# Three modulation pieces as row sums, whole-row ring places, a later overflow branch and a new order of the first latents

## The chip, the core and the metric

The program runs on one core of one Trainium2 chip. The metric is the device time of one execution in microseconds, the median of several runs; less is better. TensorE (PE), VectorE (DVE), ScalarE (ACT), GpSimd (POOL) and SyncE (SP, which only issues DMAs here) run their own instruction queues and meet at semaphores.

## What is computed

Two blocks, on 256 latent tokens and 256 context tokens of width 1024, all in fp32. The first has two layers; each takes a modulation vector `silu(c) @ ada_w + ada_b` of 6 x 1024 numbers (shift, scale and gate of the mixer, then of the FFN), one for the latents and one for the context:

```python
sh1, sc1, g1, sh2, sc2, g2 = split(silu(c) @ ada_w[i] + ada_b[i], 6)
h  = x * (1 + sc1) + sh1                                    # modulate
x  = layer_norm(ALPHA * x + g1 * mixer(h), ln1_g, ln1_b)    # i=0: MLA, i=1: neighbourhood
h  = x * (1 + sc2) + sh2
x  = layer_norm(ALPHA * x + g2 * conv_ffn(h), ln2_g, ln2_b) # 2816 hidden, depthwise conv, SiLU gate
```

The second block is a mixer of several branches on the latents and a hierarchical mixture of 32 experts, each token going to a few of them; an expert holds 6 MB of weights (`w_moe`), 201 MB in all.

## The kernel before

**Exact products.** A weight is loaded as `raw`, copied to a rounded high part `wh` by ACT (L122), and the rest `wl` is a subtraction on DVE or POOL in turn (L125, counted by `lo_turn`). `mm3` (L136 to L138) makes each product of three matmuls. The activations have high and low parts too (`ah`/`al`, `hh`/`hl`).

**Modulation of layer 0** is made on PE in 12 pieces of 512 columns: `ada_mm` loads a piece as 8 tiles `wa` of 256 KB (L184) and multiplies them with silu(c) (L186), ACT evicts (L189), `ada_fin` turns it (L195), sums over four row groups (L197) and adds the bias (L199). Pieces 0 to 3 (shift and scale of the mixer) are made in the head, 4 to 11 inside the attention pipeline, one every two steps.

**Modulation of layer 1** is made on DVE: `rows()` loads 128 rows of the transposed matrix (L225) and sums `row * silu(c)` along each row by one `scalar_tensor_tensor` with an accumulator (L228). There are 64 such jobs; they are given out three at a time after each hidden block j of layer 0's FFN (`filler`, AR = 3).

**Head.** `modulated` loads half of `xT` (L528), makes h (L537), its parts, and scales `xT` by ALPHA on POOL (L541) for the later residual. `latent` makes the q latents (384 wide, four 128-token tiles in four PSUM banks), then the kv latents (288 wide). Their order on PE, with the modulation pieces between, is written out by hand (`in_order`).

**Attention, outputs, FFN.** The MLA attention runs as a software pipeline of 16 steps. `outputs` makes the mixer's output projection block by block (m = 0 to 7) with a residual on DVE (L422), then the layer norm. The FFN goes through its 22 hidden blocks j in three thirds (8, 8, 6), each followed by an output phase over m.

**Expert weights** come in 192 pieces of 1 MB through a ring of 19 places in SBUF, issued by `fetch` (L1405) on SP, at most eight in flight. Two of the places are the halves of `xT`, which is free by then: `xT[:, :, 256:]` and `xT[:, :, :256]` of a tile [128, 8, 512], so that a partition's 8 KB lie there as eight rows of 1 KB. The other 17 places take 8 KB in a row. After expert `OVER_AT` = 7 stands a branch (L1654, L1655) for the case that an expert has more than 32 tokens; it is not taken with these inputs. SP passes it too, in its own queue.

The rest of the order is left to a scheduler that keeps the written order where it is told to (`keep_in_program_order`).

## Time and profile before

| | |
|---|---|
| median of 3 runs | 1931.78 us (1931.07 to 1932.93) |
| profiled execution | 1928.94 us, of which span of the core 1927.1 us |
| busy, share of the span | PE 87%, DVE 51%, ACT 39%, POOL 25% |
| granted PE clock, mean | 0.931 |

The span runs from the first instruction to the last; an engine's share is its busy time over the span, as an average over stages with different limits. Read by stage: the head with the first latents is 0 to 91 us, the attention pipeline 92 to 250, the MLA outputs 250 to 292, layer norm and FFN of layer 0 from 293 on (its first third of hidden blocks ends near 410), and the experts from about 1464 to 1915. The clock is the one that the throttle granted, as a share of full speed.

### The profile page before, as it was taken

The page shows a single profiled execution, that of the slowest core. Times are in us where ns is not written, and L with a number is a line of the kernel's source. Part 1 is how long each engine was busy: PE and PEld are TensorE (multiplying, and loading weights), DVE is VectorE, ACT ScalarE, POOL GpSimd, SP SyncE. Part 2 cuts the span into 40 slices and gives each one's busy share as a digit, 9 for nine tenths or more (in the row PEclk, how much of TensorE's full clock was granted, in tenths as well). Part 3 has the DMA queues.
Part 4 walks back from the last instruction along what each step waited for, and adds up shares of the span by engine and source line. Part 5 has one row for each costly group of instructions (what it writes and reads, how often), then busy time and mean ns, then how long its engine had stood idle before and what let it go on. Part 6 is the DMA issues. An engine that isn't in the chain of part 4 may idle for free. (4 is left out here: it accounts for less than half of the span.)

```text
span 1927.1 us, 29718 instructions
## 1 busy us (share of the span) xinstructions
PE 1677.7 (87%) x11807; PEld 1273.8 (66%) x11807; DVE 991.9 (51%) x1927; ACT 742.4 (39%) x1395; POOL 476.1 (25%) x313
## 2 busy tenths in 40 slices
PE   6899998989999989999899978997988676766666
PEld 3778776868878768887899966676965232322322
DVE  4478837873764756665756565668533111100101
ACT  2577744422432444554556543454522010100101
POOL 3344523211211233222444343023421000000000
PEclk8999999999999999999999999899999877877878
DMA  7333441443654533222365546131667999999997
GB/s 285 98 115 121 164 142 55 156 150 103 202 196 133 172 111 131 92 96 96 126 187 183 178 151 218 64 107 43 257 252 300 412 378 412 412 411 412 412 412 295
DMA packets 109966, 396.89 MB, mean 206 GB/s; under 512 B 11008, under 2 KB 33536, under 8 KB 87552
## 3 DMA queue, kind: packets, MB, share of 16 engines
q1 hardware_dynamic: 109536, 394.44, 55.9%
q8 instruction: 94, 1.54, 0.3%
q10 hardware_dynamic: 288, 0.52, 0.1%
q14 instruction: 48, 0.39, 0.1%
HBM read 393.87 MB, written 1.05 MB: 205 GB/s over the span
## 5 line engine op out<-in xcount | busy, mean ns | idle before, releaser
L125 POOL TENSOR_TENSOR wl<-raw,wh 128x1024 fp32r<-128x1024 f32 (+3 forms) x133 | 310.0, 2332 | 670.0 <-ACT wh L122 555.5
L122 ACT ACTIVATE wh<-raw 128x1024 fp32r<-128x1024 f32 (+4 forms) x256 | 259.8, 1017 | 344.2 <-PE mm L137 246.0
L137 PE MATMUL mm<-ah,wh 128*128 128x256 f32 (+1 forms) x888 | 302.0, 341 | 2.8 <-POOL ah L343 2.5
L136 PE MATMUL mm<-ah,wh 128*128 128x256 f32 (+1 forms) x888 | 297.3, 342 | 4.8 <-ACT ah L342 4.1
L138 PE MATMUL mm<-ah,wl 128*128 128x256 f32 (+1 forms) x888 | 298.6, 338 | 2.1 <-DVE wl L125 1.1
L125 DVE TENSOR_TENSOR wl<-raw,wh 128x1024 fp32r<-128x1024 f32 (+4 forms) x123 | 155.7, 1266 | 83.3 <-ACT wh L122 82.9
L1574 PE MATMUL mm<-mw,xg 128*32 128x256 f32 x1792 | 139.1, 443 | 66.8 <-DMA mw<-in_w_moe_dram 65.0
L136 PEld LDWEIGHTS mm<-ah,wh 128*128 128x128 f32 x888 | 167.0, 191 | 31.5 <-ACT ah L342 5.7
L137 PEld LDWEIGHTS mm<-ah,wh 128*128 128x128 f32 x888 | 169.2, 191 | 27.7 <-POOL ah L343 8.8
L138 PEld LDWEIGHTS mm<-ah,wl 128*128 128x128 f32 x888 | 169.1, 191 | 22.6 <-DVE wl L125 1.8
L1574 PEld LDWEIGHTS mm<-mw,xg 128*32 128x32 f32 x1792 | 58.0, 122 | 145.4 <-DMA mw<-in_w_moe_dram 83.7
L1580 DVE TENSOR_TENSOR mg<-mm,mg 64x256 f32<-64x256 f32 x32 | 13.6, 426 | 231.6 <-ACT mg L1579 231.5
L136 PE MATMUL mm<-hh,wh 128*128 128x256 f32 (+1 forms) x364 | 121.9, 337 | 7.4 <-ACT hh L837 7.3
L138 PE MATMUL mm<-hh,wl 128*128 128x256 f32 (+1 forms) x364 | 121.5, 335 | 0.0
L137 PE MATMUL mm<-hl,wh 128*128 128x256 f32 (+1 forms) x364 | 121.4, 335 | 0.0
L422 DVE SCALAR_TENSOR_TENSOR xT<-mm,mod,xT 128x256 f32<-128x256 f32 x96 | 44.0, 481 | 135.9 <-PE mm L138 135.7
L1594 PE MATMUL mm<-mw,mhT 128*32 128x256 f32 x944 | 83.0, 498 | 19.6 <-DMA mw<-in_w_moe_dram 6.4
L1579 ACT ACTIVATE mg<-mm 64x256 f32<-64x256 f32 x32 | 12.1, 377 | 215.2 <-PE mm L1574 215.2
L1618 DVE COPY my<-mm 32x256 f32<-32x256 f32 x64 | 26.8, 418 | 123.3 <-PE mm L1594 107.9
L1556 POOL TENSOR_TENSOR OW<-OH,cw 128x256 f32<-128x256 f32 x8 | 4.9, 615 | 337.5 <-PE tr L1561 331.4
L1616 ACT ACTIVATE my<-mm 32x256 f32<-32x256 f32 x64 | 24.0, 375 | 164.4 <-DVE my L1618 160.4
L228 DVE SCALAR_TENSOR_TENSOR junk<-row,cb 128x1024 f32<-128x1024 f32 x64 | 86.5, 1351 | 0.0
(542 smaller groups left out, 3755.9 us busy)
## 6 DMA issues: line engine op xcount, KB each, us to landing
mw<-in_w_moe_dram SPq DMA_DIRECT2D x171, 1024.0 KB, 19.8
raw<-in_ffn_w_in_dram SPq DMA_DIRECT2D x88, 512.0 KB, 3.3
wa<-in_ada_w_dram SPq DMA_DIRECT2D x96, 256.0 KB, 4.2
row<-in_ada_r_dram SPq DMA_DIRECT2D x48, 512.0 KB, 4.4
xT<-in_w_moe_dram SPq DMA_DIRECT2D x21, 1024.0 KB, 20.7
raw<-in_ffn_w_out_dram SPq DMA_DIRECT2D x32, 512.0 KB, 3.9
raw<-in_w_merge_dram SPq DMA_DIRECT2D x16, 512.0 KB, 3.6
raw<-in_ffn_w_out_dram SPq DMA_DIRECT2D x16, 384.0 KB, 3.2
```

The costliest lines, as they stand in the source:

```text
L122: self.nc.scalar.activation(h[:, :n], raw[:, :n], AF.Copy)
L125: eng.tensor_tensor(l[:, :n], raw[:, :n], _f(h)[:, :n], op=OP.subtract)
L136: mm(out, l[0], r[0], start=start, stop=False)
L137: mm(out, l[0], r[1], start=False, stop=False)
L138: mm(out, l[1], r[0], start=False, stop=stop)
L228: nc.vector.scalar_tensor_tensor(junk, self.row, 1.0, self.cb[:, s], op0=OP.mult, op1=OP.mult, accum_out=self.mod[1][:, f, s:s + 1]))
L422: self.nc.vector.scalar_tensor_tensor(v, p, self.mod[i][:, 8 * c_g + m, s:s + 1], v, op0=OP.mult, op1=OP.add)
L1574: nc.tensor.matmul(p[32 * j:32 * j + 32, :256], xg[:, k, sl_e], w[:, j], start=k == 0, stop=k == 7, tile_position=(0, 32 * j))
L1580: V.tensor_tensor(g, p[64:128, :256], g, op=OP.mult)
L1594: nc.tensor.matmul(p[32 * j:32 * j + 32, :256], hT[:, f % 2, f // 2], w[:, j], start=f == 0, stop=f == 3, tile_position=(0, 32 * j))
L1616: nc.scalar.activation(o, p[32 * j:32 * j + 32, :256], AF.Copy)
L1618: V.tensor_copy(o, p[32 * j:32 * j + 32, :256])
```

## The change

1. **Head.** Pieces 0 to 3 are regrouped (`ada_0`): piece g holds shift and scale for feature blocks 2g and 2g+1, in two DMAs of 1 MB; `xT` comes in four pieces. A piece is made, its two blocks of h follow, and the q latents of all four token tiles and the kv latents of tiles 0 and 1 are multiplied at once, step by step. The kv latents of tiles 2 and 3 follow in a second pass (`rest`), for which the four kv weights are loaded and split again. Eight matmuls that compute nothing (`keep_warm`, `WU0`) stand behind the first piece. The scaling by ALPHA on POOL is gone: the gate pieces 4 and 5 are divided by ALPHA instead, and the layer norm takes `LN_EPS / ALPHA ** 2`.
2. **Row sums.** Pieces 9 to 11 of layer 0 leave PE (`AJ = 9`); pieces 4 to 8 go into the attention pipeline, one every three steps. The 24 row sums that replace the three pieces go ahead of layer 1's 64: eight in the MLA outputs (`AO`), then three after a hidden block but not after the last two of a third, and two after each m of the output phases of the first and second third (`AM`).
3. **Ring places.** `xT` becomes [128, 2, 8, 256]: each half is 8 KB in a row.
4. **Branch.** `OVER_AT` goes from 7 to 29; its body uses ring places as its buffers.

```diff
-WA, AR = 4, 3
+WA, AJ, AO, AR, AM = 4, 9, (2, 2, 1, 1, 1, 1, 0, 0), 3, 2
+WU0 = 8
-OVER_AT = 7
+OVER_AT = 29
-        self.xT = c.tile([128, 8, 512], F, name="xT")
+        self.xT = c.tile([128, 2, 8, 256], F, name="xT")
...
@@ ada_mm
+        if j < 4:
+            w = self.wa.tile([128, 4, 512], F, name="wa")
+            nc.sync.dma_start(out=w, in_=self.d["ada_0"][j, half])
...
@@ ada_fin
+        if j in (4, 5):
+            nc.vector.tensor_scalar(m, m, 1.0 / ALPHA, None, op0=OP.mult)
...
@@ rows_begin
-        self.row_jobs = [(f, s) for f in range(48) for s in range(2 if f < 16 else 1)]
+        self.row_jobs = [(0, f, s) for f in range(4 * AJ, 48) for s in range(2)]
+        self.row_jobs += [(1, f, s) for f in range(48) for s in range(2 if f < 16 else 1)]
...
@@ outputs
             part(m, weights(m), self.bank("mm")[:, :256 * halves], 0, halves)
+            if each:
+                each(m)
...
@@ modulated
-            nc.gpsimd.tensor_scalar(self.xT[:, m], self.xT[:, m], ALPHA, None, op0=OP.mult)
...
@@ mla
-            with self.psum(mm=6, tr=2):
-                with self.pool("wa0", 19) as self.wa, self.in_order():
-                    self.ada(0)
-                    self.ada(2)
-                    self.modulated(0, early)
-                    ...
-                    ps = latent("mla_wq", 384, (2, 2, 2, 2), rest)
+            with self.psum(mm=8):
+                with self.pool("wa0", 4) as self.wa, self.in_order():
+                    ...
+                    def both(g, e):
+                        latent(g, e, "mla_wq", psq)
+                        latent(g, e, "mla_wkv", psk)
+                    def rest(g):
+                        W.pop(("mla_wkv", g))
+                        for e in range(2):
+                            latent(g, e, "mla_wkv", psr)
+                    ada(0)
+                    self.keep_warm("mm", WU0, self.cs.rearrange("p a b -> p (a b)"))
+                    psq = {t: self.bank("mm") for t in range(4)}
+                    psk = {t: self.bank("mm") for t in range(2)}
+                    both(0, 0)
+                    ada(1)
+                    both(0, 1)
+                    for g in range(1, 4):
+                        if g < 3:
+                            ada(g + 1)
+                        for e in range(2):
+                            both(g, e)
+                    psr = {t: self.bank("mm") for t in range(2, 4)}
+                    for g in range(4):
+                        rest(g)
...
-                for j in range(8):
-                    if j:
-                        at(2 * j, self.ada_fin, 3 + j)
-                    at(2 * j, self.ada_mm, 4 + j, 0)
-                    at(2 * j + 1, self.ada_mm, 4 + j, 1)
+                for j in range(4, AJ):
+                    u = 3 * (j - 4) + 1
+                    at(u, self.ada_mm, j, 0)
+                    at(u + 1, self.ada_mm, j, 1)
+                    at(u + 2, self.ada_fin, j)
...
@@ ffn
-                    if filler:
-                        filler.pop(0)()
+                    if filler and j < j1 - 2:
+                        filler(AR)
...
                         self.residual(m, p[:, 256 * s:256 * s + 256], i, 5, s)
+                    if filler:
+                        filler(AM)
...
@@ first
+        self.rows_begin()
-        self.outputs(..., ln(("ln1_g", 0), ("ln1_b", 0), ALPHA, GB))
+        self.outputs(..., norm, each=lambda m: self.rows(AO[m]))
-        self.rows_begin()
-        self.ffn(0, 512, after, [lambda: self.rows(AR)] * HT)
+        self.ffn(0, 512, after, self.rows)
...
@@ moe
-                    self.rings += [self.xT[:, :, :256]]
+                    self.rings += [self.xT[:, 0]]
```

**SP's queue in the experts.** Before, SP's rows from the ring's first lap to the branch (`mw` and `xT` are the pieces by their place; L1654 and L1655 are the branch):

```order
194 L1405 DMA mw<-in_w_moe_dram 128x2048 x6
195 L1405 DMA xT<-in_w_moe_dram 128x8x256 x2
196 L1405 DMA mw<-in_w_moe_dram 128x2048 x17
197 L1405 DMA xT<-in_w_moe_dram 128x8x256 x2
198 L1405 DMA mw<-in_w_moe_dram 128x2048 x12
199 L1654 TENSOR_LOAD most_i
200 L1655 COMPARE_AND_BRANCH
```

In the changed kernel the same queue near its end (the branch is L1689 and L1690 now):

```order
235 L1439 DMA xT<-in_w_moe_dram 128x2048 x2
236 L1439 DMA mw<-in_w_moe_dram 128x2048 x17
237 L1439 DMA xT<-in_w_moe_dram 128x2048 x2
238 L1439 DMA mw<-in_w_moe_dram 128x2048 x10
239 L1689 TENSOR_LOAD most_i
240 L1690 COMPARE_AND_BRANCH
```

and what stands behind the branch and its body:

```order
271 L1690 UNCONDITIONAL_BRANCH
272 L1655 DMA fn<-in_final_norm_dram 128x1024
273 L1439 DMA mw<-in_w_moe_dram 128x2048 x7
274 L1439 DMA xT<-in_w_moe_dram 128x2048 x2
275 L1439 DMA mw<-in_w_moe_dram 128x2048
```

The pieces in `xT` go out as 128 whole rows, and the branch has moved from among the first pieces to ten pieces before the last.

**DVE at the end of the FFN's first third.** Before, the rows of the last two hidden blocks (L228 is a row sum, L838 makes `hl`, which PE waits for with `hh`, L422 is the first residual of the output phase):

```order
485 L228 SCALAR_TENSOR_TENSOR junk,mod_88<-row,cb 128x1024
486 L125 TENSOR_TENSOR wl<-raw,wh 128x1024
487 L228 SCALAR_TENSOR_TENSOR junk,mod_88<-row,cb 128x1024
488 L828 SCALAR_TENSOR_TENSOR u_4235<-mm,cols,u_4235 128x2x255
489 L228 SCALAR_TENSOR_TENSOR junk,mod_88<-row,cb 128x1024
490 L830 SCALAR_TENSOR_TENSOR u_4235<-mm,cols,u_4235 128x2x255
491 L828 SCALAR_TENSOR_TENSOR u_4239<-mm,cols,u_4239 128x2x255
492 L830 SCALAR_TENSOR_TENSOR u_4239<-mm,cols,u_4239 128x2x255
493 L835 TENSOR_TENSOR sg<-sg,u_4235 128x512
494 L838 TENSOR_TENSOR hl<-sg,hh 128x512
495 L228 SCALAR_TENSOR_TENSOR junk,mod_88<-row,cb 128x1024
496 L422 SCALAR_TENSOR_TENSOR xT<-mm,mod_87,xT 128x256
```

In the changed kernel the same place (L248 is the row sum, L865 makes `hl`, L441 is the residual):

```order
496 L855 SCALAR_TENSOR_TENSOR u_4135<-mm,cols,u_4135 128x2x255
497 L857 SCALAR_TENSOR_TENSOR u_4135<-mm,cols,u_4135 128x2x255
498 L127 TENSOR_TENSOR wl<-raw,wh 128x1024
499 L855 SCALAR_TENSOR_TENSOR u_4139<-mm,cols,u_4139 128x2x255
500 L857 SCALAR_TENSOR_TENSOR u_4139<-mm,cols,u_4139 128x2x255
501 L862 TENSOR_TENSOR sg<-sg,u_4135 128x512
502 L865 TENSOR_TENSOR hl<-sg,hh 128x512
503 L441 SCALAR_TENSOR_TENSOR xT<-mm,mod_87,xT 128x256 x2
504 L248 SCALAR_TENSOR_TENSOR junk,mod_88<-row,cb 128x1024 x2
505 L441 SCALAR_TENSOR_TENSOR xT<-mm,mod_87,xT 128x256 x2
506 L248 SCALAR_TENSOR_TENSOR junk,mod_88<-row,cb 128x1024
```

No row sum stands between the last two hidden blocks now; they resume between the residuals of the output phase.

## Rows read from the trace of the kernel before

**Rows 1.** The page's chain of work that ended last, shares of the span by line.
```profile
DMA mw<-in_w_moe_dram 15%; DMA xT<-in_w_moe_dram 2%; PE mm L1574 0%; PE acc L1625 0%; PE mm L1594 0%; PE gt L1547 0%; DVE xg L1552 0%; SPq L1405 0%; DVE my L1618 0%; PE tr L1583 0%; ACT my L1616 0%; ACT out L1644 0%; ACT t L1635 0%; DVE out L1636 0%; PE tr L1547 0%
```
**Rows 2.** Busy time by stage: window, length, PE, PEld, DVE, ACT, POOL, clock, DMA, GB/s.
```profile
92.00:250.00 158.00, 149.89 (x998) 120.78 (x997) 129.09 (x270) 116.49 (x272) 76.50 (x63) 0.98 0.39 131
250.00:292.00 42.00, 42.00 (x229) 33.90 (x227) 10.44 (x19) 14.88 (x17) 8.45 (x4) 1.00 0.41 145
300.00:340.00 40.00, 35.59 (x193) 26.88 (x192) 37.84 (x83) 19.84 (x37) 17.25 (x19) 0.96 0.20 67
340.00:410.00 70.00, 70.00 (x301) 56.26 (x300) 62.12 (x80) 27.86 (x38) 19.39 (x7) 1.00 0.47 155
420.00:500.00 80.00, 80.00 (x343) 64.30 (x342) 38.74 (x60) 23.70 (x28) 16.79 (x7) 1.00 0.38 125
```
**Rows 3.** Timeline of PE in the head: start, length, what, wait before it.
```profile
13.41 3.99 PE L186 MATMUL mm<-wa,cs 128*32 128x512 f32 x16
18.09 0.66 PE L195 MATMUL tr<-ident,t 128*128 128x128 f32 x4 [0.69 <-ACT t L189]
21.60 0.69 PE L136 MATMUL mm<-wh,ah 128*128 128x384 f32 x1 [2.86 <-ACT wh L122]
23.83 0.52 PE L138 MATMUL mm<-wh,ah 128*128 128x384 f32 x1
28.10 0.34 PE L137 MATMUL mm<-wl,ah 128*128 128x384 f32 x1
28.28 0.34 PE L138 MATMUL mm<-wh,ah 128*128 128x384 f32 x1
29.60 1.92 PE L186 MATMUL mm<-wa,cs 128*32 128x512 f32 x16
44.86 0.69 PE L137 MATMUL mm<-wl,ah 128*128 128x384 f32 x1 [3.04 <-DVE wl L125]
54.81 0.29 PE L136 MATMUL mm<-wh,ah 128*128 128x288 f32 x1
54.94 0.29 PE L137 MATMUL mm<-wl,ah 128*128 128x288 f32 x1
```
**Rows 4.** PE's waits, 92 to 250 us, the longest sum: total, times, longest.
```profile
PE tr L633 <- DVE PTl L144: 5.0, 5, 1.6
```
**Rows 5.** Timeline of PE at the end of the FFN's first third.
```profile
417.17 0.79 PE L136 MATMUL mm<-hh,wh 128*128 128x512 f32 x1 [6.58 <-ACT hh L837]
...
418.62 0.63 PE L137 MATMUL mm<-hl,wh 128*128 128x512 f32 x1
...
420.58 0.39 PE L137 MATMUL mm<-hl,wh 128*128 128x512 f32 x1
420.81 0.39 PE L138 MATMUL mm<-hh,wl 128*128 128x512 f32 x1
```
**Rows 6.** All row sums: duration in ns (min/median/max), first and last start.
```profile
L228 DVE SCALAR_TENSOR_TENSOR junk<-row,cb x64: 1207/1216/3422, 336.6 to 666.7; 128x1024 f32<-128x1024 f32 x64
```
**Rows 7.** Windows in the experts, columns as in rows 2.
```profile
1640.00:1654.00 14.00, 9.81 (x102) 3.97 (x98) 1.36 (x4) 0.75 (x2) 0.00 (x0) 0.67 1.01 420
1654.00:1668.00 14.00, 8.73 (x89) 4.87 (x82) 2.29 (x5) 0.99 (x3) 0.00 (x0) 0.88 1.05 391
...
1544.00:1550.00 6.00, 5.85 (x19) 3.02 (x18) 0.12 (x1) 0.00 (x0) 0.00 (x0) 0.77 0.45 149
```
**Rows 8.** The page's DMA packets, and its issues of ring pieces (count, size, us to landing).
```profile
DMA packets 109966, 396.89 MB, mean 206 GB/s; under 512 B 11008, under 2 KB 33536, under 8 KB 87552
...
mw<-in_w_moe_dram SPq DMA_DIRECT2D x171, 1024.0 KB, 19.8
...
xT<-in_w_moe_dram SPq DMA_DIRECT2D x21, 1024.0 KB, 20.7
```
**Rows 9.** The branch's line: instructions, duration in ns, first and last start.
```profile
L1655 SPq EVENT_SEMAPHORE  x8: 17/17/17, 1535.0 to 1547.6; - x8
```
**Rows 10.** The page's costliest groups, the residuals: busy us, mean ns, idle before.
```profile
L422 DVE SCALAR_TENSOR_TENSOR xT<-mm,mod,xT 128x256 f32<-128x256 f32 x96 | 44.0, 481 | 135.9 <-PE mm L138 135.7
```

More of the change, by code (lines that the diff above doesn't have):

```diff
@@ L413, in last_norm, with outputs @@
             n = self.tmp()[:, :256]
[L414 removed]
+            V.tensor_tensor(n, self.xT[:, 0, m], p[:, 0], op=OP.mult)
             V.tensor_tensor(n, n, p[:, 1], op=OP.subtract)
[L416 removed]
+            nc.scalar.activation(self.xT[:, 0, m], n, AF.Identity, scale=self.col(("ln2_g", 1), m, 1),
                                  bias=self.col(("ln2_b", 1), m, 1))
     def residual(self, m, p, i, c_g, s):
[L421 removed]
+        v = self.xT[:, s, m]
         self.nc.vector.scalar_tensor_tensor(v, p, self.mod[i][:, 8 * c_g + m, s:s + 1], v, op0=OP.mult, op1=OP.add)
[L424 removed]
+    def outputs(self, weights, acts, i, c_g, halves, after, w=None, each=None):
         n = len(acts)
@@ L666, in qt_ @@
                 q_turn(g, t, X.pop((g, t)))
-            def latent(w, n, ks, between=None):
-                ps = [self.bank("mm") for _ in range(4)]
-                k = 0
-                for ci, kn in enumerate(ks):
-                    wh, wl = early[w, ci] if (w, ci) in early else self.weight(d[w][ci][:, :kn * n], kn, n)
-                    for e in range(kn):
-                        for t in range(4):
-                            self.mm3(ps[t][:, :n], (self.ah[k][:, tsl(t)], self.al[k][:, tsl(t)]),
-                                     (wh[:, e], wl[:, e]), k == 0, k == 7)
-                        k += 1
-                        if between:
-                            between(k)
-                return ps
             def normed(ps, part, feats):
@@ L706, in turned, with latent @@
                     self.hilo(hi[:, f], lo[:, f], p, self.col(norm, f, 1))
-            with self.psum(mm=6, tr=2):
-                wa = self.wa
-                with self.pool("wa0", 19) as self.wa, self.in_order():
-                    self.ada(0)
-                    self.ada(2)
-                    self.modulated(0, early)
-                    def rest(k):
-                        if k == 2:
-                            self.ada(1)
-                        if k == 3:
-                            self.ada(3)
-                            self.modulated(1, early)
-                    ps = latent("mla_wq", 384, (2, 2, 2, 2), rest)
+            def latent(g, e, w, ps):
+                n, k = (384 if w == "mla_wq" else 288), 2 * g + e
+                if (w, g) not in W:
+                    W[w, g] = self.weight(d[w][g], 2, n)
+                wh, wl = W[w, g]
+                for t in ps:
+                    self.mm3(ps[t][:, :n], (self.ah[k][:, tsl(t)], self.al[k][:, tsl(t)]), (wh[:, e], wl[:, e]),
+                             k == 0, k == 7)
@@ L985, in first, with norm @@
                             ((y, self.big.tile([128, 4, 512], R, name="ah", tag=f"b{i}")) for y, i in ((self.ah, 1), (self.al, 3))))
-        GB = self.affine("a", 0, 3, 4, ("ln1_g", 0), ("ln1_b", 0))
-        self.outputs(lambda m: self.weight(d["mla_wo"][m], 8, 128), acts, 0, 2, 2, ln(("ln1_g", 0), ("ln1_b", 0), ALPHA, GB))
+        self.rows_begin()
+        def norm(s):
+            if s == 0:
+                self.GBa = self.affine("a", 0, 3, 4, ("ln1_g", 0), ("ln1_b", 0))
+            return self.layernorm(s, ("ln1_g", 0), ("ln1_b", 0), ALPHA, self.GBa, True, LN_EPS / ALPHA ** 2)
+        self.outputs(lambda m: self.weight(d["mla_wo"][m], 8, 128), acts, 0, 2, 2, norm, each=lambda m: self.rows(AO[m]))
         pool.close()
-        self.rows_begin()
         def after(s):
@@ L999, in first @@
         self.na(ln(("ln1_g", 1), ("ln1_b", 1), ALPHA, GB))
-        self.rings, self.next_piece, self.pieces, self.full = [self.xT[:, :, 256:]], 0, [], False
+        self.rings, self.next_piece, self.pieces, self.full = [self.xT[:, 1]], 0, [], False
         self.fetch()
@@ L1627, in moe @@
                 if e == OVER_AT:
-                    self.overflow(most_i, over, th, tl, acc, sm, two)
+                    self.overflow(most_i, over, th, tl, acc, two, [self.rings[i % len(self.rings)] for i in (6 * e, 6 * e + 4)])
             ss, s1 = T([128, 2, 2], "fss"), T([128, 2], "fs1")
@@ L1647, in moe, with overflow @@
                     (nc.scalar if hf else nc.sync).dma_start(out=d["out"][tsl(t), c], in_=out[:, t, c])
-    def overflow(self, most_i, over, th, tl, acc, sm, two):
+    def overflow(self, most_i, over, th, tl, acc, two, places):
         nc, tc, d = self.nc, self.tc, self.d
@@ L1655, in overflow @@
         with tc.If(n > 32):
-            xT = two.tile([128, 8, 256], F, name="xg", bufs=1)
+            xT, ws = [r.tile([128, 8, 256], F, name="mw", tag=tag) for r, tag in places]
             for t in range(2):
```

107 lines of the change are left out of this document (56 added, 51 removed).

## The prediction

> **What bounds the kernel now.** I read the chain of work that ended last first, then the busy time by stage, then PE's waits and timelines inside the stages that the change touches. The chain [rows 1] hangs on DMA alone: the ring pieces, `mw` with 15% and `xT` with 2% of the span. That holds for the experts only, since the chain ends there; in the experts DMA moves 420 GB/s [rows 7], and only a higher rate or a shorter interruption helps. Ahead of them PE is the bound, with exceptions that matter here. In the attention pipeline PE is busy for 149.9 of 158 us and DVE for 129 [rows 2]; in the MLA outputs PE never rests and DVE has 31 of 42 us free; from 300 to 410 us DVE is busy for 37.8 of 40 and 62.1 of 70 us, with PE full from 340 on; in the output phase and the hidden blocks that follow DVE is at half. So DVE is the second bound in the FFN's first third, and nowhere else in the part that is changed.
>
> All terms go against the profiled execution, 1928.94 us, which is 2.8 us under the median of 1931.78.
>
> **Head: 5.5 us less.** Before, two pieces (0 and 2) stand ahead of the first latent matmul, which starts at 21.60 [rows 3]. Piece 0 was done, turned included, when piece 2 began at 13.41. Now piece 0 alone stands ahead, but with 512 KB of `xT` in the queue before it, 1.2 us at 420 GB/s, so it is done near 14.6. From the end of piece 2's turn (18.09 + 0.66) to the first latent matmul the old kernel took 2.85 us; the same again gives 17.5, that is 4.1 us earlier. In exchange three pieces instead of two lie between the latents, and one costs PE 1.92 + 0.69 (wait for ACT's eviction) + 0.66 = 3.3 us: 0.8 us remain. Then the wait of 3.04 us for a `wl` at 44.86 should go: POOL had the scaling by ALPHA in its queue, which is removed, and the weights come in smaller splits. After that wait the matmuls ran at the lower clock, 0.52 us instead of 0.34 [rows 3], about eleven of them; starts are 0.32 us apart there against 0.18 at 28.10, so 1.5 us. Sum 0.8 + 3.0 + 1.5 = 5.3, taken as 5.5. The number of latent matmuls stays (96 of each width). The second pass splits and loads four kv weights again, on ACT, DVE or POOL and SP; it hides as long as PE has the first pass to do, 96 x 0.18 + 48 x 0.13 = 23.5 us plus the three pieces' 10. The eight warming matmuls fill the wait for h and cost nothing. Ends: 0, if the extra splits give a wait like the 3.04 again and eat the rest; 10, if the 2.86 us wait at 21.60 shrinks and the slow stretch behind it goes too.
>
> **Attention pipeline: 5.5 us less.** Three pieces leave PE: 3 x (1.92 + 0.66) = 7.7 us at most. PE is at 95% there, so most of it should show; but PE already waits 5.0 us for DVE's `PTl` [rows 4], and if that doubled, 2.7 would be left. DVE stays below PE (129 against 142). Nearer the upper end: 5.5.
>
> **MLA outputs: nothing.** Eight row sums of 1.22 us [rows 6] are 10 us on a DVE with 31 us free. Their four row loads (512 KB each) and the 1 MB of `silu(c)` rows go through SP beside weights at 145 of 420 GB/s. Cover gone, a row sum ahead of a residual would cost 1.2 us each, 10 us at worst. Three small operations that make the layer norm's factors now follow the sums, below 1 us.
>
> **FFN, first third: 7 us less.** At the end of the third PE waits 6.58 us for `hh` and `hl` of the last hidden block [rows 5], since DVE is behind; then about seven matmuls run at the low clock, 0.63 instead of 0.39 us (0.2 us each in step), 1.4 us: 8 us in all. Before, 24 row sums lie there, three per hidden block up to the last; now 18, none in the last two blocks, as DVE's order shows. Six sums of 1.22 us are 7.3 us off the engine that is late, more than the 6.58. I take 7; the ends are 8, and 2 if the sums still run behind. What is late next is PE itself. The sums moved to the output phases find room: an m takes PE 24 x 0.23 = 5.6 us [rows 5], and DVE there does two sums and two residuals, 2 x 1.22 + 2 x 0.48 [rows 6, 10], with half of the `wl` splits some 4 us. The tail of the sums, 88 instead of 64, still ends before the FFN does.
>
> **Ring places: 9.5 us less.** Windows of 14 us show 420 GB/s without and 391 with a pair of `xT` pieces in flight [rows 7]: 14 x (1 - 391/420) = 0.97 us per pair. There are 21 such pieces [rows 8], ten pairs: 9.7 us. Their packets are the odd ones: 171 x 512 = 87552 are those of `mw`, just the count under 8 KB, while 21 x 1024 = 21504 of those under 2 KB are `xT`. Whole rows make an `xT` piece like an `mw` piece. The low end comes from landing times, 20.7 against 19.8 us: 0.9 us for each of 21 pieces with eight in flight, 21 x 0.9 / 8 = 2.4 us. The drop of the rate is the nearer measurement, since DMA is the bound itself: 9.5.
>
> The Trainium skill, on the page "DMA: Bandwidth & Descriptors", section "Why small descriptors are slow (HBM only)", puts the price of a packet at about three cycles beside one cycle per 32 bytes. By that a packet of 1 KB costs 35 cycles for 32 and one of 2 KB 67 for 64, and the saving would be an estimated 21 x 0.11 = 2.4 us instead of 9.5. No row above confirms the rule; the drop to 391 GB/s speaks for more.
>
> **Branch: nothing.** SP waits at the branch until all eight outstanding pieces have landed [rows 9], and DMA falls to 149 GB/s for 6 us [rows 7], a hole of 6 x (1 - 149/420) = 3.9 us. In the changed order ten pieces and `fn` still stand behind the branch, so SP drains the queue again, later. The hole moves and stays. Ends: 4 us less if it hides at the end, 4 us more if the eight pieces of the drain and the last ten cannot overlap with what PE still has to do.
>
> **Sum:** 5.5 + 5.5 + 7 + 9.5 = 27.5 us; 1928.94 - 27.5 = 1901.4 profiled, and with the 2.8 us **1904 us** as the median.
>
> **Rivals.**
> - *Less in ring and head.* The rate in a lap with `xT` pieces has other causes than the rows' length, and 2.4 us is all; the head's second pass makes DVE and ACT late and the head gives nothing. For it: the landing times differ by 0.9 us only. Against it: the dips come with the pairs. 1904 + 7 + 5.5 = 1917 us. The Trainium skill's price of a packet, above, would agree with the first half. Chance 0.13.
> - *The hole at the branch goes too.* The change then does more than the order shows: 1904 - 4 = 1900 us. For it, ten pieces only are left to delay; against it, the same drain stands in SP's queue. Chance 0.08.
> - *The head stays at the low clock.* PE fell to it after waits of 2.86 and 3.04 us [rows 3]. If the waits for each h keep PE there through the first pass and the second, 96 x 0.14 + 96 x 0.10 + 4 x 2.1 is 31 us, less some 9 that the old head lost so too: 22 more, and the 5.5 lost: 1904 + 27 = 1931 us, no change. Against it: from 28 us on the old head held 0.34 through a piece in between. Chance 0.06.
> - *Slower: row sums held up by POOL.* The longest row sum takes 3.42 us against 1.22 [rows 6], and beside it POOL was splitting a weight. In the output phases of two thirds (16 m) DVE needs 2r + 1.0 for sums of length r and residuals, and some 0.6 for splits, against PE's 5.6: from r = 2.0 us on DVE is late there, and from r = 2.7 us on the loss, 16 x (2 x 2.7 + 1.6 - 5.6) = 22 us, outweighs the gains outside the FFN (20.5 us). At 3.42 it is 45 us: 1904 + 7 + 45 = 1956 us. Against it: half of the 64 sums take 1.216 us or less, and POOL is busy for 16.8 of 80 us there [rows 2]. The Trainium skill ("SBUF — State Buffer", section "Who interferes with whom") says that a VectorE instruction with two SBUF inputs and a GpSimd one that reads SBUF exclude each other for a whole instruction, which speaks against adding such sums; the 3.42 us agree, the median says that it is rare. Chance 0.05.
>
> **How the numbers follow.** The forecast, all four gains near their values, has 0.66; with the rivals' 0.13, 0.08, 0.06 and 0.05, the 0.02 left lie evenly about no change. About 0.2%, 3.9 us, is what a measurement of this kernel can tell from no change. Faster: 0.66 + 0.13 + 0.08 = 0.87; same 0.07; slower 0.06. The ends of the terms together (head 0 to 10, attention 2.7 to 7.7, FFN 2 to 8, ring 2.4 to 9.7, branch 4 either way) rarely fall on one side; the range takes the second rival in fully, the first to its value, and some 10 us of the terms below the forecast: 1894 to 1918.
>
> **What would show it.** Right: the kv latents end about 5 us earlier; no piece of 256 KB in the pipeline after five; no wait of several us for `hh` between the first hidden third and its outputs; the experts' rate at 420 GB/s through laps with `xT` pieces; a hole of 4 us near the end. Wrong: matmuls of 0.52 us after 30 us; row sums with a mean over 2 us; a dip to 391 GB/s twice a lap; waits for a residual's bank in the output phases.

## The result, and the profile after

The changed kernel takes 1908.14 us (median of four runs, 1903.61 to 1911.99) against 1932.36 for the kernel before on the same chip: a ratio of 0.9869, with an interval of 0.984 to 0.9898, so 20 to 31 us less. The forecast was 1904, in a range from 1894 to 1918. The profiled execution is 1908.82 us, 20.1 us under the one of before, with a span of 1907.0. Single runs of one kernel lie up to 14 us apart on a chip, so parts of a few us are read from the traces, stage by stage. Even there the same stage with the same code differs from profile to profile by 1 to 3 us, the second block's mixer by up to 7. A stage ends at the start of one instruction that both kernels have; the table gives the stage's length in each profile.

| stage, and what ends it (line of before) | before | after | difference | forecast |
|---|---|---|---|---|
| head and attention, last turned P (L633) | 247.2 | 239.3 | -7.9 | -11.0 |
| MLA outputs, first operation of the layer norm (L335) | 55.3 | 56.7 | +1.4 | 0 |
| layer norm, FFN's first third, 8th `hh` (L837) | 114.0 | 108.8 | -5.2 | -7.0 |
| rest of layer 0's FFN, last `hh` (L837) | 248.9 | 250.1 | +1.2 | 0 |
| neighbourhood attention and its layer norm (L347) | 274.6 | 277.7 | +3.1 | 0 |
| layer 1's FFN, last residual (L422) | 186.8 | 193.9 | +7.1 | 0 |
| second block's mixer, first expert matmul (L1574) | 332.9 | 322.5 | -10.4 | 0 |
| experts, last copy of an output (L1618) | 456.9 | 447.1 | -9.8 | -9.5 |
| end | 10.5 | 10.9 | +0.4 | 0 |

So the total hides large terms that the prediction had not priced, in stages whose code is not touched, and they nearly cancel: 11.4 us lost from the second third of layer 0's FFN to the end of layer 1's FFN, 10.4 won behind it.

The experts first. Windows of the changed kernel (columns as in [rows 2]), two full laps, then the branch's hole near the end:

```profile
1600.00:1625.00 25.00, 14.79 (x164) 5.71 (x164) 3.08 (x8) 1.88 (x5) 0.00 (x0) 0.80 1.01 420
1650.00:1675.00 25.00, 19.59 (x216) 10.57 (x212) 3.15 (x8) 4.00 (x10) 1.23 (x2) 0.96 1.01 420
...
1850.00:1860.00 10.00, 5.86 (x62) 2.42 (x58) 0.72 (x2) 0.38 (x1) 0.00 (x0) 0.67 0.94 392
1860.00:1865.00 5.00, 2.85 (x28) 1.04 (x24) 0.84 (x2) 0.75 (x2) 0.00 (x0) 0.50 0.30 123
```

The dips to 391 GB/s [rows 7] are gone, and DMA stops once, at 1860 us. The page's packets and its ring issues, beside [rows 8]:

```profile
DMA packets 87485, 398.06 MB, mean 209 GB/s; under 512 B 10544, under 2 KB 11568, under 8 KB 61616
...
mw<-in_w_moe_dram SPq DMA_DIRECT2D x171, 1024.0 KB, 19.8
...
xT<-in_w_moe_dram SPq DMA_DIRECT2D x21, 1024.0 KB, 19.8
```

Under 2 KB there are 21968 packets fewer, the 21504 of the `xT` pieces among them, and an `xT` piece lands as fast as an `mw` piece. The counts are cumulative, as these rows show: 87485 - 61616 = 25869 packets of 8 KB and more, about 192 x 128, so every piece is 128 packets of 8 KB. The prediction read the 87552 of before as 171 x 512, which fits by accident only.

The branch's line, to be held against [rows 9]: SP drains its eight queues again, now up to 1864 us.

```profile
L1690 SPq EVENT_SEMAPHORE  x8: 17/17/17, 1856.6 to 1864.3; - x8
```

In the head, PE's timeline shows the warming matmuls (L155), the first latent matmul and the second piece:

```profile
12.79 1.94 PE L194 MATMUL mm<-wa,cs 128*32 128x512 f32 x8 [0.43 <-DMA wa<-in_ada_dram]
15.53 1.08 PE L203 MATMUL tr<-ident,t 128*128 128x128 f32 x4 [0.81 <-ACT t L197]
16.41 5.57 PE L155 MATMUL mm<-cs,ident 128*128 128x256 f32 x16
21.63 0.53 PE L138 MATMUL mm<-wh,ah 128*128 128x384 f32 x1
...
24.81 1.92 PE L194 MATMUL mm<-wa,cs 128*32 128x512 f32 x16
```

and ACT's timeline the first parts of h (`ah`, two of 0.64 us each):

```profile
20.07 1.28 ACT L554 ACTIVATE ah<-t 128x512 fp32r<-128x512 f32 x2 [3.38 <-DVE t L552]
```

The first latent matmul starts at 21.63, not at the 17.5 of the forecast and no earlier than before [rows 3]; in ten other profiles with the same head it starts at 18.7 to 21.2. Three things make up these 4.1 us. The first piece's matmuls now wait for two loads of 1 MB, the second of which lets PE on at 12.79, and piece 0 is turned at 16.6 instead of 14.6: 2.0 us. Its `ah` is there 4.1 us behind that turn, at 20.7, and not 2.85 us: 1.3. The warming matmuls hold PE 0.9 us longer still. PE's last kv latent and its first matmul of the scores show what is won behind that and what is lost again. Before:

```profile
67.39 0.29 PE L138 MATMUL mm<-wh,ah 128*128 128x288 f32 x1
...
91.65 0.50 PE L136 MATMUL sc<-kx,qT 128*128 128x512 f32 x1 [2.74 <-DVE V L478]
```

and in the changed kernel:

```profile
64.12 0.29 PE L140 MATMUL mm<-wh,ah 128*128 128x288 f32 x1
...
89.71 0.50 PE L138 MATMUL sc<-kx,qT 128*128 128x512 f32 x1 [2.00 <-DVE V L499]
```

The kv latents end 3.3 us earlier, the scores start 1.9 us earlier. In between PE waits 2.3 us for a query on VectorE, where it waited 1.0 before, and from 75.07 to 78.16 us it runs at a granted clock of 0.50, the lower level, which the kernel before does not do there.

PE's waits in the attention pipeline, the longest sums (before: [rows 4]):

```profile
PE tr L646 <- DVE PTl L146: 4.4, 6, 1.5
PE tr L646 <- DVE adar L205: 1.8, 1, 1.8
PE tr L203 <- DVE qT L146: 1.7, 1, 1.7
PE tr L656 <- DVE adar L205: 1.6, 2, 0.8
```

The last three are new, 5.1 us together, and belong to the pieces that are left: PE stands behind their sum (`adar`) and ahead of their turn.

At the end of the FFN's first third the wait is shorter than before (6.58 [rows 5]), but still there. PE's waits from 250 to 420 us:

```profile
PE mm L138 <- ACT hh L864: 4.4, 1, 4.4
```

and all row sums, beside [rows 6]:

```profile
L248 DVE SCALAR_TENSOR_TENSOR junk<-row,cb x88: 1206/1216/3376, 252.3 to 641.3; 128x1024 f32<-128x1024 f32 x88
```

Why VectorE is late although no row sum stands in the last two blocks: DVE's timeline inside the first third, where `hl` (L865) takes 0.69 us when nothing holds it up,

```profile
360.58 2.49 DVE L865 TENSOR_TENSOR hl<-sg,hh 128x512 fp32r<-128x512 f32 x1 [0.78 <-ACT hh L864]
362.99 1.21 DVE L248 SCALAR_TENSOR_TENSOR junk<-row,cb 128x1024 f32<-128x1024 f32 x1
```

and POOL's at the same time:

```profile
360.11 2.41 POOL L127 TENSOR_TENSOR wl<-raw,wh 128x1024 fp32r<-128x1024 f32 x1 [9.71 <-ACT wh L124]
```

The split on POOL runs until 362.5, and `hl` ends half a us behind it, 1.8 us late. That comes in five of the eight hidden blocks of this third (again at 372.62, beside a split at 372.15). A block then takes 12.0 us from one `hh` to the next (371.97 to 384.02), while PE needs 48 x 0.235 = 11.3; the five blocks together are 3.5 us longer than that, most of the 4.4 us. In the second third the same happens to a row sum. DVE, then POOL:

```profile
489.44 2.76 DVE L248 SCALAR_TENSOR_TENSOR junk<-row,cb 128x1024 f32<-128x1024 f32 x1
```

```profile
488.69 2.43 POOL L127 TENSOR_TENSOR wl<-raw,wh 128x1024 fp32r<-128x1024 f32 x1 [9.52 <-ACT wh L124]
```

In the MLA outputs the first operation of the layer norm (L354) is late. DVE's timeline:

```profile
294.56 1.23 DVE L127 TENSOR_TENSOR wl<-raw,wh 128x1024 fp32r<-128x1024 f32 x1
...
296.03 0.41 DVE L354 TENSOR_TENSOR t<-xT,acc 128x256 f32<-128x256 f32 x1
```

A weight split stands ahead of it on DVE. In the kernel before, POOL makes that split (at 302.71), and the layer norm begins at 302.45 without it.

**Theory.** Weights take turns between DVE and POOL by one counter for the whole kernel (`lo_turn`); only in the attention pipeline do all go to POOL. The second pass of the kv latents added five splits (eight kv weights instead of three), an odd number. Every later weight whose low part was made on POOL is now made on DVE, and the other way. That decides in each stage which VectorE operation meets a split on POOL, and which split PE waits for; it would explain the stages whose code is the same. The rivals: the row sums load the FFN whatever meets them, and the untouched stages differ by chance.

### The profile page after: what moved, and what is told of

It reads as the page before. It is cut to its first block, busy times and chain, and to the rows that moved or that the text cites. A ratio compares the mean times of both kernels' runs of the same rounds, so it can differ in the third digit from the quotient of the medians.

```text
span 1907.0 us, 29628 instructions
## 1 busy us (share of the span) xinstructions
PE 1655.7 (87%) x11763; PEld 1271.2 (67%) x11763; DVE 1070.1 (56%) x1990; ACT 742.7 (39%) x1397; POOL 465.4 (24%) x306
## 2 busy tenths in 40 slices
DMA packets 87485, 398.06 MB, mean 209 GB/s; under 512 B 10544, under 2 KB 11568, under 8 KB 61616
## 5 line engine op out<-in xcount | busy, mean ns | idle before, releaser
L127 POOL TENSOR_TENSOR wl<-raw,wh 128x1024 fp32r<-128x1024 f32 (+4 forms) x134 | 312.7, 2334 | 687.4 <-ACT wh L124 637.5
L127 DVE TENSOR_TENSOR wl<-raw,wh 128x1024 fp32r<-128x1024 f32 (+3 forms) x127 | 161.1, 1269 | 71.3 <-ACT wh L124 68.8
L248 DVE SCALAR_TENSOR_TENSOR junk<-row,cb 128x1024 f32<-128x1024 f32 x88 | 136.0, 1545 | 5.8 <-ACT cb L231 3.9
L441 DVE SCALAR_TENSOR_TENSOR xT<-mm,mod,xT 128x256 f32<-128x256 f32 x96 | 43.7, 480 | 85.2 <-PE mm L140 85.0
```

The source lines that it names most:

```text
L127: eng.tensor_tensor(l[:, :n], raw[:, :n], _f(h)[:, :n], op=OP.subtract)
L248: nc.vector.scalar_tensor_tensor(junk, self.row, 1.0, self.cb[:, s], op0=OP.mult, op1=OP.mult, accum_out=self.mod[i][:, f, s:s + 1]))
L441: self.nc.vector.scalar_tensor_tensor(v, p, self.mod[i][:, 8 * c_g + m, s:s + 1], v, op0=OP.mult, op1=OP.add)
```

## The experiments

Each kernel was profiled and timed against the kernel before on the same chip. Stage lengths are those of the table above.

### The ring places alone

The kernel before with the layout of `xT` and nothing else:

```diff
-        self.xT = c.tile([128, 8, 512], F, name="xT")
+        self.xT = c.tile([128, 2, 8, 256], F, name="xT")
...
-                    self.rings += [self.xT[:, :, :256]]
+                    self.rings += [self.xT[:, 0]]
```

> The kernel before with nothing but the new layout of xT, so that the two ring places in it take whole rows. Theory (packets of 1 KB slow the ring): the windows of the experts move 420 GB/s in every lap, the experts from their first matmul to the end are 9.7 us shorter, and the whole is 9 to 10 us below the kernel before, about 1922. Rival (landing time only, or the price of a packet by the page on DMA): 2.4 us, about 1929. Second rival (the stage gained from the later branch or the earlier start instead): the dips to 391 GB/s in laps with xT pieces stay.

Measured: 1922.16 us against 1934.18, ratio 0.993 (0.9915 to 0.9945). The experts take 447.1 us instead of 456.9, 9.8 less, as in the changed kernel. (Two stages that the ring does not touch show how far profiles differ: the neighbourhood attention takes 276.8 us against 274.6 before, the mixer 335.5 against 332.9.) Two windows of 25 us, one lap and the next:

```profile
1600.00:1625.00 25.00, 18.06 (x172) 7.30 (x172) 3.11 (x8) 2.26 (x6) 0.00 (x0) 0.80 1.01 421
...
1650.00:1675.00 25.00, 18.23 (x162) 9.52 (x155) 4.54 (x10) 3.45 (x8) 0.62 (x1) 0.87 1.02 422
```

The term stands, alone and whole. The Trainium skill's price of a packet ("DMA: Bandwidth & Descriptors", "Why small descriptors are slow (HBM only)") gives, for packets of 1 KB in place of 8 KB, an estimated 8% or 0.2 us per piece, 4.2 us for 21. The run shows 9.8: rows of 1 KB cost more than twice this estimate.

### The branch: left out, and early again

```diff
-                if e == OVER_AT:
+                if e == NE:
```

> The changed kernel without the branch for overfull experts (its body is left out too; no expert here has more than 32 tokens, so nothing that is computed changes). Theory (the hole was only moved, and its full length is still on the path): DMA never stops before the last piece, and the time falls by the hole, 4 to 5 us. Rival (a hole ten pieces before the end is partly hidden behind PE): under 2 us.

Measured: 1907.78 us, ratio 0.9863 (0.9848 to 0.9878), not to be told from the changed kernel's 0.9869. DMA does not stop:

```profile
1850.00:1885.00 35.00, 22.93 (x226) 8.48 (x215) 3.94 (x10) 3.01 (x8) 0.00 (x0) 0.71 1.01 421
```

and the experts take 444.7 us, 2.4 less than 447.1 (446.5 to 448.7 in the profiles of all other runs with whole rows). The hole costs about half of what was expected; that the median shows none of it is within its scatter (the mixer ahead was 3.6 us longer in this profile, with the same code).

The branch after expert 7 again, its body with buffers of its own:

```diff
-OVER_AT = 29
+OVER_AT = 7
```

> The changed kernel with the branch after expert 7 again, its body with buffers of its own as before. Theory (the place of the branch is worth nothing): the hole of 4 to 5 us stands near 1533 us instead of 1862, and the time is within 1 us of the changed kernel. Rival (the late place hides part of it): 2 to 4 us slower than the changed kernel.

Measured: 1906.61 us, ratio 0.9858 (0.9843 to 0.9874); the experts take 447.3 us. The hole is back in front:

```profile
1530.00:1533.00 3.00, 3.00 (x8) 1.12 (x7) 0.17 (x1) 0.38 (x1) 0.00 (x0) 1.00 0.72 295
1533.00:1539.00 6.00, 5.85 (x46) 4.51 (x44) 1.38 (x2) 1.20 (x2) 0.00 (x0) 1.00 0.52 197
```

The place of the branch is worth nothing, as forecast.

### The warming matmuls

```diff
-WU0 = 8
+WU0 = 0
```

> The changed kernel without the eight matmuls that compute nothing behind the first modulation piece. They end at 21.6 us in the changed kernel, where the first latent matmul begins without a wait. Theory (they keep the clock up and cost less than they save): the first latent matmul starts up to 1 us earlier, at 20.7 or so, but runs at 0.52 us instead of 0.34 for the next 6 us, so the first probabilities come 1 to 3 us later than at 91.6. Rival (they only stand in the way): the first latent matmul starts about 1 us earlier, later ones at full clock, and the time is about 1 us less.

Measured: 1910.94 us, ratio 0.9878 (0.9863 to 0.9893), within the scatter. PE's timeline:

```profile
14.92 1.09 PE L203 MATMUL tr<-ident,t 128*128 128x128 f32 x4 [0.81 <-ACT t L197]
20.14 0.69 PE L138 MATMUL mm<-wh,ah 128*128 128x384 f32 x1 [4.13 <-ACT ah L554]
20.63 0.52 PE L139 MATMUL mm<-wl,ah 128*128 128x384 f32 x1
...
25.81 1.92 PE L194 MATMUL mm<-wa,cs 128*32 128x512 f32 x16
```

After a wait of 4.13 us the latents take 0.52 us for 5 us. That is their length in [rows 3], where the granted clock is 0.50 (23.8 to 27.7 us); that it is the lower clock here too is read from the lengths alone, since the profile's row for this stretch names 1.00. The turn of piece 0 starts 0.6 us earlier in this profile than in the changed kernel's (14.92 against 15.53). So of the 1.5 us by which the latents start earlier 0.9 are the warming's, which outlasts the wait for h by as much, and from that turn to the second piece it takes 10.9 us here and 9.3 with the warming: eight matmuls on nothing save 1.6 us up to there. Nothing of that is left at the first probabilities, by which the expectation was stated:

```profile
L484 ACT ACTIVATE P<-sc,mx x64: 457/574/695, 91.1 to 237.6; 128x512 f32<-128x512 f32 x32, 128x256 f32<-128x256 f32 x32
```

They start at 91.1 us, not 1 to 3 us later than the 91.6 of the changed kernel; the stretch at the lower clock from 75.07 us on is missing here. The ten other profiles with the warming have 89.0 to 91.2. So the theory holds up to the second piece, and that the warming pays in the end is not shown.

### The three pieces back on PE

```diff
-WA, AJ, AO, AR, AM = 4, 9, (2, 2, 1, 1, 1, 1, 0, 0), 3, 2
+WA, AJ, AO, AR, AM = 4, 12, (0, 0, 0, 0, 0, 0, 0, 0), 3, 2
```

with the pieces one every two steps again.

> The changed kernel with pieces 9 to 11 of layer 0 back on PE in the attention pipeline, one every two steps, and no row sum in the MLA outputs (64 sums in the FFN, by the new places). Theory: the attention pipeline is 6 to 7 us longer, the MLA outputs 1 us shorter, and layer 0's FFN at most 2 us shorter: 4 to 6 us slower than the changed kernel in all. Rival (24 sums more cost the FFN as much as PE saved): within 1 us of the changed kernel.

Measured: 1913.66 us, ratio 0.9914 (0.9887 to 0.9941), 5 us slower by the medians and 9 by the ratios. Head and attention end at 243.0 us instead of 239.3; the outputs (56.8) and the time from the layer norm to the last `hh` (359.7 against 358.9) are the same. So the three pieces are worth 3.7 us at the end of the attention, and their 24 sums cost nothing that shows. The remaining 4.2 of the 7.9 us are not the head's alone: the scores start only 1.9 us earlier (91.65 to 89.71). PE's busy time from the first matmul of the scores to the end of the attention, in the changed kernel and in this run:

```profile
89.71:239.30 149.59, 136.54 (x925) 113.65 (x926) 126.00 (x264) 114.31 (x268) 72.08 (x61) 1.00 0.30 96
```

```profile
89.01:243.00 153.99, 145.49 (x980) 116.15 (x981) 128.63 (x273) 116.18 (x272) 75.45 (x62) 1.00 0.41 134
```

The three pieces take 9.0 us of PE's time with them, but the stretch is only 4.4 us shorter (not 3.7, as this run's scores start 0.7 us earlier): 4.6 us became waits, and those for `adar` and `qT` above, 5.1 us, are not among this run's.

### The turn of the splits

From the MLA outputs on:

```diff
         self.rows_begin()
+        self.lo_turn += 1
```

> The changed kernel with the turn of the weight splits moved by one from the MLA outputs on, so that every weight whose low part went to POOL now goes to DVE and the other way, as it was in the kernel before (the five added kv splits had moved the turn by one). Theory (the turn decides which row sums meet a split on POOL, and which split PE waits for): row sums of layer 0's second and third thirds are back at 1.22 us mean instead of 1.6 to 1.7, a hidden block there takes 11.25 us instead of 11.7 to 12.2; layer 1's FFN is 7 us shorter, and the mixer behind it gives up to 10 us back as in the kernel before: between 3 us less and 5 us more in all. Rival (the row sums are many, whatever meets them): the stages keep their lengths within 1 us each.

Measured: 1909.53 us, ratio 0.9876 (0.9851 to 0.9901). The sums of the second and third thirds are back at a mean of 1.22 us, as expected. Nearly every stage from the outputs on goes back towards the length it had before, the neighbourhood attention by half: outputs 55.1, rest of layer 0's FFN 247.5, layer 1's attention with its layer norm 276.1, layer 1's FFN 188.5, mixer 336.1. The total barely moves, as the gains and the loss cancel; the FFN's first third, 108.8, is as long with either turn. For layer 1's FFN alone:

```diff
+            self.lo_turn += 1
             self.ffn(1, 256, None)
+            self.lo_turn += 1
```

> The changed kernel with the turn of the weight splits moved by one for layer 1's FFN alone, and back behind it. Theory (the turn made that FFN 7 us longer, and the mixer behind it is faster on its own account): 5 to 7 us less than the changed kernel, about 1902. Rival (what the FFN gains the mixer gives back, since both wait for the same thing, the weights' loads or the clock): within 2 us of the changed kernel.

Measured: 1905.89 us, ratio 0.9856 (0.9829 to 0.9882). The total lies about 2 us under the changed kernel, within the scatter, so it decides nothing; the stages do. That FFN takes 187.7 us instead of 193.9; the mixer stays short, 325.2 (320 to 326 in all runs with this turn there, 333 to 336 in those with the other). PE's waits in that FFN, in the changed kernel,

```profile
PE mm L138 <- ACT hh L864: 3.3, 3, 1.4
PE mm L140 <- POOL wl L127: 2.8, 2, 2.0
```

and in this run:

```profile
PE mm L138 <- ACT hh L864: 0.7, 2, 0.3
...
PE mm L140 <- POOL wl L127: 0.4, 1, 0.4
```

So 5 of the 6.2 us are waits for a split on POOL and for an `hh`. In the mixer a wait of the same kind shows with the other sign; in the kernel before, from 1130 to 1200 us,

```profile
PE pj L137 <- POOL wl L125: 5.1, 3, 2.6
```

and in the changed kernel:

```profile
PE pj L139 <- POOL wl L127: 1.1, 1, 1.1
```

That is 4.0 us, but other waits grew, and in sum PE's idle time in the mixer is only 3.4 us shorter. The larger part is PE's clock. The whole mixer, before and in the changed kernel:

```profile
1126.80:1459.70 332.90, 289.60 (x2074) 239.00 (x2071) 208.31 (x425) 151.90 (x313) 107.56 (x65) 0.93 0.44 156
```

```profile
1126.50:1449.00 322.50, 282.63 (x2080) 233.74 (x2080) 206.23 (x425) 152.19 (x315) 106.64 (x65) 0.96 0.45 161
```

PE is busy 7.0 us less with the same matmuls, at a mean granted clock of 0.96 instead of 0.93. The three runs with the turn of before have 0.93 and 289.6 to 290.7 us there, the eleven with the other turn 0.94 to 0.96 and 281.3 to 287.4. That the mixer follows the turn is shown by these runs; which wait brings the lower clock stays open. For layer 0's FFN alone:

```diff
+        self.lo_turn += 1
         self.ffn(0, 512, after, self.rows)
+        self.lo_turn += 1
```

> The changed kernel with the turn of the weight splits moved by one for layer 0's FFN alone. Theory (collisions of row sums with POOL splits follow from the turn): the mean of the row sums in the second third falls from 1.73 to 1.2 us, that third from 80.0 to 78.7 us between the same points, while the first third gets the collisions instead, with a longer wait at its end than 4.4 us: within 3 us of the changed kernel. Rival (the turn does not matter for the sums): means and stages as in the changed kernel.

Measured: 1905.04 us, ratio 0.9858 (0.9833 to 0.9884). The second third falls from 80.0 to 78.7 us, its sums from a mean of 1.73 to 1.22 us. The first third gets the colliding sums (mean 1.49), as expected, and its `hl` takes 0.69 us throughout, but the wait at its end shrinks to 1.4 us instead of growing; that part of the expectation was wrong. The third itself is as long as in the changed kernel (108.8 us), so a late sum costs it as much as a late `hl`; PE's wait is shorter since PE begins the output matmuls at 401.8 us here, ahead of the last `hh` at 403.6. The outputs go back to 55.2 us: the split that stood ahead of the layer norm on DVE is POOL's now (at 295.04), and the layer norm begins ahead of it:

```profile
294.84 0.41 DVE L354 TENSOR_TENSOR t<-xT,acc 128x256 f32<-128x256 f32 x1
```

### No split on GpSimd beside the row sums

```diff
+        self.lo_pool = 10 ** 9
         self.ffn(0, 512, after, self.rows)
+        self.lo_pool = LO_POOL
```

> The changed kernel with all low parts of layer 0's FFN weights made on VectorE, none on GpSimd. Theory (each split on GpSimd holds up one VectorE operation with two inputs, hl in the first third and a row sum later, by 1.5 to 1.8 us): the longest row sum in that FFN falls from 3.4 to 1.22 us, its hl takes 0.69 us everywhere instead of 2.49 in the first third, and although VectorE takes 22 blocks and 24 outputs of splits more at 1.22 us each, the FFN is no longer than in the changed kernel, 1 to 3 us shorter from first normalisation to the last hidden block. Rival (row sums take 1.6 us for other reasons, their loads or their place): the sums stay at 1.6 us, VectorE is overloaded and the FFN is 10 us longer.

Measured: 1904.13 us, ratio 0.9854 (0.983 to 0.9877). From the layer norm to the last `hh` 352.6 us instead of 358.9, more than expected; the first third is 3.5 us shorter (105.3), and the wait at its end is gone. (The total is not to be told from the changed kernel's.) All row sums:

```profile
L248 DVE SCALAR_TENSOR_TENSOR junk<-row,cb x88: 1212/1217/1226, 253.9 to 635.1; 128x1024 f32<-128x1024 f32 x88
```

None is over 1.23 us, and PE is never idle from 340 to 410 us, with POOL idle:

```profile
340.00:410.00 70.00, 70.00 (x300) 56.09 (x299) 59.57 (x92) 28.54 (x37) 0.00 (x0) 1.00 0.48 151
```

In the changed kernel the same window was:

```profile
340.00:410.00 70.00, 65.64 (x274) 52.39 (x273) 58.85 (x76) 25.04 (x34) 13.44 (x6) 0.98 0.47 149
```

DVE makes twice the splits and is busy hardly longer: what it did besides was waiting for POOL, counted as busy. This settles the cause inside that FFN. It agrees with the Trainium skill ("SBUF — State Buffer", "Who interferes with whom"): of a VectorE operation with two inputs in SBUF and a GpSimd one that reads there, one waits for the whole of the other; in the two pairs above the split had started first, and `hl` and the sum ended 0.6 and 1.1 us behind it.

### Each stage with its better turn

The turn moved by one ahead of layer 0's FFN, and again behind layer 1's:

```diff
+        self.lo_turn += 1
         self.ffn(0, 512, after, self.rows)
...
             self.ffn(1, 256, None)
+            self.lo_turn += 1
```

> The changed kernel with the turn of the weight splits moved by one from layer 0's FFN to the end of layer 1's FFN, and back for the mixer behind it: each stage has the turn that was the shorter one. Theory (stages add): layer 0's FFN with its layer norm 4 us less as in the run that turned it alone, the neighbourhood attention 1.5 us less, layer 1's FFN 6 us less, the rest unchanged: 11 us under the changed kernel, about 1897. Rival (what a stage gains is given back in the next): within 4 us of the changed kernel.

Measured: 1895.96 us, ratio 0.9813 (0.9789 to 0.9837), some 11 us under the changed kernel. The stages add: outputs 55.1, layer norm and FFN of layer 0 356.3, layer 1's FFN 186.6, mixer 321.5. On top of it, more sums in the outputs:

```diff
-WA, AJ, AO, AR, AM = 4, 9, (2, 2, 1, 1, 1, 1, 0, 0), 3, 2
+WA, AJ, AO, AR, AM = 4, 9, (2, 2, 2, 2, 2, 2, 2, 2), (2, 3, 3), 2
```

> As the run before it, with sixteen row sums in the MLA outputs instead of eight, and two instead of three after each hidden block of the FFN's first third. Theory (the sums after a hidden block make VectorE the bound there): no wait for hh is left at the end of the first third, 1 to 3 us less than the run before it; the outputs keep their length. Rival (VectorE has no room left in the outputs beside GpSimd's splits): the outputs are 2 to 4 us longer and nothing is gained.

Measured: 1894.14 us, ratio 0.9802 (0.9779 to 0.9826), not to be told from the run before it. Only twelve sums went into the outputs, since their last two m run in another loop, so this run leaves out two of the 88 sums. The first third is 1.6 us shorter, no wait for `hh` is left at its end, and the outputs keep their length (55.3): the direction is the theory's, and the total lies within the scatter. Last, the turn and no split on GpSimd in layer 0's FFN together:

```diff
+        self.lo_turn, self.lo_pool = self.lo_turn + 1, 10 ** 9
         self.ffn(0, 512, after, self.rows)
+        self.lo_pool = LO_POOL
...
             self.ffn(1, 256, None)
+            self.lo_turn += 1
```

> The changed kernel with both mendings that made a stage shorter: the turn of the weight splits moved by one for the neighbourhood attention and layer 1's FFN and back behind it, and no split on GpSimd in layer 0's FFN. Theory (the stages add): outputs, normalisation and FFN of layer 0 as in the run without splits on GpSimd there, attention and FFN of layer 1 as in the run that turned both layers: 2 us under that run, 12 to 14 us under the changed kernel, about 1894. Rival (both cure the same lateness of VectorE, one behind the other): no less than the run that turned both layers.

Measured: 1894.07 us, ratio 0.9811 (0.9794 to 0.9829), the same ratio as with the turn alone. Layer norm and FFN of layer 0 are down to 352.5 us, as in the run without splits, but the outputs are back at 56.7 and layer 1's attention is 1.7 us longer, so about 0.5 us is left of the 2. The outputs show why at one place: with no split on POOL, the one ahead of the layer norm is DVE's again (295.13, the layer norm at 296.60). So the rival holds in the total, but not for its reason, since layer 0's FFN did gain 3.8 us beyond the turn; why layer 1's attention is longer stays open. This kernel and the one with the turn alone beat both kernels, the changed one by 11 to 14 us.

## Why the prediction was right, and where not

The time, 1908, lies in the range, and the direction is right. That it came so near the forecast is partly luck: of the 27.5 us that were forecast the profiles show 22.9 in their places, and the stages that were priced at nothing lost 13.2 us and won 10.4. Step by step:

- **Ring places: right.** 9.5 forecast, 9.8 measured alone and in the whole. The working has one error, the packets of an `mw` piece (128 of 8 KB, not 512 of 2 KB); the sum did not hang on it.
- **Branch: right.** The hole moved and stayed, as SP's order showed. Its price was taken too high, 3.9 us against 2.4 by the run without it.
- **Head: 1.9 instead of 5.5 where the scores start.** The step that failed is "it is done near 14.6" with the first latent at 17.5: in pieces of 1 MB PE starts only when a whole half has landed, h took 4.1 us behind the turn and not 2.85, and the warming matmuls, which were to "cost nothing", outlast the wait for h by 0.9 us. What paid is the rest of that term: the wait of 3.04 us and the slow stretches behind both old waits are gone, and the kv latents end 3.3 us earlier, not 5. Of that, 1.4 us go again in a longer wait for a query and at a lower clock, of which the prediction has nothing.
- **Attention: 4.4 instead of 5.5 by the pieces.** They took 9.0 us of PE's time with them, more than the 7.7 of the sum, but new waits at the remaining pieces' own sums and turns ate 4.6. The prediction weighed a longer wait for `PTl` only, and that did not grow (4.4 us against 5.0). Head and attention together gave 7.9 of 11 us; 1.9 by the head and 4.4 by the pieces leave 1.6 us that no run isolates.
- **FFN's first third: 5.2 instead of 7.** Fewer sums did shorten the wait, 4.4 us against 6.58, but "since DVE is behind" was put down to their number alone. In the kernel before, the 21 sums of that third have a mean of 1.63 us, not 1.22: 8.7 us of it are waiting for POOL. In the changed kernel five `hl` wait for POOL there, 1.8 us each, and without splits on POOL the third is another 3.5 us shorter.
- **"MLA outputs: nothing", and the stages not named: wrong.** The outputs lost 1.4 us, not by the sums (the run without sums there has the same 56.8): one of the FFN's first weights is split on DVE ahead of the layer norm, 1.23 us, and with that split on POOL the outputs take 55.2. Layer 1's FFN lost 7.1 us and the mixer won 10.4, both by the turn of the splits. The neighbourhood attention's 3.1 us are less sure: the kernel before and the run with the ring places alone differ by 2.2 there with the same turn, and turning the splits back gave 1.6. The diff shows it: three kv weights become eight, and a counter that hands out every second split goes through the whole kernel. The prediction counted these splits as load in the head, and not as a step of the counter.
- **The rivals.** "Row sums held up by POOL" was the right mechanism at a small size: means of 1.6 to 1.75 us from the first third's outputs on, below the 2.0 from which it was to bind there. "Less in ring and head" fell with the ring's 9.8 us, though the head did give less, and "the hole goes too" fell with the drain at 1860 us; and the head did not stay at the low clock, its latents take 0.34 us from 22 us on.
- **The signs.** Of those for right, the rate in the laps, the hole near the end and the five pieces came as named; the kv latents end 3.3 us earlier, not 5, and a wait of 4.4 us for `hh` stayed. Of those for wrong one came, matmuls of 0.52 us behind 75 us, though not in the latents.

## What to carry to other kernels

Where work is dealt out in turn by a counter, one piece of work more or less changes every later assignment: look at its parity before comparing stages, and set it anew for each stage. Two engines that hold each other up can be worth keeping apart where one of them is nearly full, even if that gives the fuller one more to do: layer 0's FFN was 6.3 us shorter so. Whole rows as the destination of large transfers are worth a change of layout where DMA is the bound.

## What the runs showed of the hardware

- Rows of 1 KB in two of nineteen places cost 9.8 us over 21 pieces of 1 MB, 0.47 us each beside the 2.5 us that a piece takes at 420 GB/s.
- A VectorE operation that meets a split on GpSimd that had started first ends about its own length after the split (started at 489.44, ended at 492.2, the split at 491.1), and the profile counts the wait as busy time: 2.76 us for a sum of 1.22.
- At a branch that is not taken SP waits for all eight DMAs in flight: DMA falls to 123 GB/s for 5 us, and the experts are 2.4 us shorter without the branch.
- The same matmuls of the mixer kept PE busy for 282.6 us at a mean granted clock of 0.96 in the changed kernel, and for 289.9 us at 0.93 in the run that differs from it only in which engine splits which weight.
